# The first transfers of a hybrid encoder layer: gain vector first in ScalarE's queue, first weights behind x's first half in SyncE's, rounded by VectorE

## The chip, the cores and the metric

The kernel runs on one core of a Trainium2 chip. The metric is the device time of one execution in microseconds (us); before the change it is 661.3 us, the median of three runs (661.18 to 662.85).

## The reference

One layer of a hybrid encoder, on 512 tokens of width 2048, in float32:

```python
h = rms_norm(x, norm_w)
proj = jnp.einsum('bsd,de->bse', h, w_in)
q, k, v, g_attn, xr, g_lru = jnp.split(proj, SPLITS, axis=-1)
attn_out = attention_group(q, k, v, q_norm_w, k_norm_w)
lru_out = lru_group(xr, conv_w, conv_b, ...)
mixed = concatenate([rms_norm(attn_out, attn_norm_w) * silu(g_attn),
                     rms_norm(lru_out, lru_norm_w) * silu(g_lru)], axis=-1)
return x + jnp.einsum('bse,ed->bsd', mixed, w_out)
```

Only the beginning matters here: the input x, multiplied column by column by the gain `norm_w`, times a first block of 512 columns of `w_in` (those of `xr`). The factor of the norm that belongs to each token is applied later, to the product.

## The kernel before, in words

Every float32 product is made of three matmuls in a rounded format. A matrix is split into a rounded part (`wh` of the weights, `xh` of x) and a rest (`wl`, `xl`), and the products high times high, high times low and low times high are added up in PSUM. `wsplit` makes the two parts of a weight tile of 128 x 512: ScalarE rounds (`nc.scalar.copy`, L204), VectorE subtracts (L205). `xturn` (L226 to L235) transposes 128 columns of x on TensorE, four 128 x 128 pieces (L230), and from PSUM ScalarE makes `xh` (L232), scaled by the gain column `nw`, and VectorE makes `xl` (L233).

TensorE's order is written out by hand over the whole program. SyncE's is so over the first projection, and those of ScalarE and VectorE over its start. Transfers are issued from the queues of SyncE (SP) and ScalarE (ACT) at the start; `b` is the tile of a chunk of x (256 columns of all 512 tokens, 512 KB), `wr` the tile of raw weights (256 rows of `w_in` by 512 columns, 512 KB). Both firsts are loaded in two halves of 256 KB: SP issues the two halves of x's first chunk, ACT the first weight half, then `norm_w` (8 KB, into `nw_st`), then the second weight half. SP goes on with x's second chunk, the second weights and so on (L223, L193).

`nw_st` holds the gain as 16 rows; `columns` (L176 to L182) turns it with one small transpose on TensorE (L179) and copies the result to `nw` on VectorE (L181).

While the first data are on their way TensorE multiplies ones by ones: `busy(n)` issues n matmuls of 128 x 256 in bfloat16 (L924), whose result nobody reads. These are the fillers. Thirteen (`WARM`) stand ahead of the turn of the gain, six (`WARM2`) between the first transposes of x and the first real matmul. The first weights are consumed by a form of `proj_feat` of its own (L287): four matmuls of `xh` with `wh`, then x's second four transposes, then four with `wl`, four with `xl`, and the same for the second weight half. From the second chunk on the matmuls are those of `mm3` (L145 to L147). L891 and L706 belong to the output projection at the end.

The start is these lines:

```python
busy(WARM)
...
    xs, ws = xload(0, 2), wraw(w_in, 0, C_XR, 2, nc.scalar)
    xc, raw = next(xs), next(ws)
    nc.scalar.dma_start(nw_st, norm_w.rearrange("(k p) -> k p", p=P))
    next(xs), next(ws)
    ...
    columns(nw, nw_st)
    first = [wsplit(raw, 0)]
    xturn(xc, 0)
    busy(WARM2)
```

Of the kernel before, what the change touches and what calls it, by code (L numbers as in the profile page):

```python
# [16 lines left out]
P = 128  # L17
# [19 lines left out]
AHEAD = 600  # L37


WARM, WARM2 = 13, 6  # L40


STEPS = 2
# [5 lines left out]
C_Q, C_K, C_GA, C_XR, C_GL = 0, 1024, 1536, 2560, 3584  # L49
# [6 lines left out]
def hybrid_kernel(  # L56
# [20 lines left out]
    nc = tc.nc  # L77
    xf = x.rearrange("b s d -> (b s) d")
# [29 lines left out]
    def nm(s):  # L108
        cnt[0] += 1
        return f"{s}_{cnt[0]}"  # L110
# [11 lines left out]
    def b4(dt=F32, shape=(P, 2, SEQ)):  # L122
        pool, _, n = work()
        return pools[pool].tile(list(shape), dt, tag="b4", bufs=n, name=nm("b4"))
# [13 lines left out]
    def const(shape, name, dt=F32):  # L138
        return cp.tile(list(shape), dt, tag=name, name=name)

    def f(ap):
        return ap.bitcast(F32)
# [14 lines left out]
    nw_st = const([KT, P], "nw_st")  # L157
# [17 lines left out]
    def columns(dst, src):  # L175

        n = src.shape[0]
        pt = mm()
        nc.tensor.transpose(pt[:, :n], src, ident[:n, :n])  # L179
        with tc.high_priority():  # L180
            nc.vector.tensor_copy(dst, pt[:, :n])  # L181
# [2 lines left out]
        return vec[:, r : r + 1]  # L184


    def wraw(w, r0, c0, nk=1, queue=nc.sync):

        raw = pools["wr"].tile([P, 2, SEQ], F32, tag="wr", bufs=3, name=nm("wr"))
        src = w[r0 : r0 + 2 * P, c0 : c0 + SEQ].rearrange("(k p) e -> p k e", p=P)  # L190
        for k in range(nk):
            ks = slice(k * 2 // nk, (k + 1) * 2 // nk)
            queue.dma_start(raw[:, ks, :], src[:, ks, :])  # L193
            yield raw

    turn_of = [0]

    def wsplit(raw, k):

        turn_of[0] += k  # L200
        pool = pools["wx" if "wx" in pools and turn_of[0] % 2 else "xw"]
        hi = pool.tile([P, SEQ], F32R, tag="wh", bufs=4, name=nm("wh"))
        lo = pool.tile([P, SEQ], F32R, tag="wl", bufs=4, name=nm("wl"))
        nc.scalar.copy(hi, raw[:, k, :])  # L204
        nc.vector.tensor_sub(lo, raw[:, k, :], f(hi))  # L205
        return hi, lo

    def wload(w, r0, c0):
        with tc.high_priority(AHEAD):
            (raw,) = wraw(w, r0, c0)  # L210
            return [wsplit(raw, k) for k in range(2)]
# [2 lines left out]
    xh, xl = [None] * KT, [None] * KT  # L214
    ssq = const([P, NT, KT // 2], "ssq")

    def xload(c, nk=1):

        xc = b4(shape=(P, NT, 2 * P))
        for k in range(nk):  # L220
            ks = slice(k * 2 * P // nk, (k + 1) * 2 * P // nk)
            cs = slice(c * 2 * P + ks.start, c * 2 * P + ks.stop)
            nc.sync.dma_start(xc[:, :, ks], xf[:, cs].rearrange("(t p) d -> p t d", p=P))  # L223
            yield xc

    def xturn(xc, kk):  # L226
        pt = mm()
        for t in range(NT):
            ks = slice(kk % 2 * P, (kk % 2 + 1) * P)
            nc.tensor.transpose(pt[:, t * P : (t + 1) * P], xc[:, t, ks], ident)  # L230
        xh[kk], xl[kk] = x2(), x2()
        nc.scalar.activation(xh[kk], pt, AF.Identity, scale=nw[:, kk : kk + 1])  # L232
        nc.vector.scalar_tensor_tensor(  # L233
            xl[kk], pt, nw[:, kk : kk + 1], f(xh[kk]), op0=ALU.mult, op1=ALU.subtract
        )  # L235
# [8 lines left out]
    def xchunk(c):  # L244
        with tc.high_priority(AHEAD):
            (xc,) = xload(c)
        yield
        with tc.high_priority(AHEAD):
            for k in range(2):
                xturn(xc, 2 * c + k)  # L250
        xsquare(xc, c)
        yield
# [669 lines left out]
    def busy(n):  # L922
        for _ in range(n):
            nc.tensor.matmul(warm[:, : 2 * P], wv[:, :P], wv, start=True, stop=True)  # L924
# [8 lines left out]
    )  # L933
    given = {}
    with tc.high_priority():
        xs, ws = xload(0, 2), wraw(w_in, 0, C_XR, 2, nc.scalar)
        xc, raw = next(xs), next(ws)
        nc.scalar.dma_start(nw_st, norm_w.rearrange("(k p) -> k p", p=P))
        next(xs), next(ws)
        table = const([P, 1], "table")  # L940
        nc.scalar.activation(table, ones[:, :1], AF.Exp)
        columns(nw, nw_st)
        first = [wsplit(raw, 0)]
        xturn(xc, 0)
        busy(WARM2)
    chunks = [xchunk(c) for c in range(1, KT // 2)]
    loads, turns = iter(chunks), iter(chunks)
    for step in proj_feat(C_XR, a1, first, given):
        if step is None:
            with tc.high_priority():  # L950
                first.append(wsplit(raw, 1))
                xturn(xc, 1)
            xsquare(xc, 0)
            next(next(loads), None)
            given[1] = wload(w_in, 2 * P, C_XR)
            continue
        c, e = step
        if (e == 0 or e == 2) and c:
            next(next(loads, iter(())), None)
        if (e, c) == (2, 0) or (e == 1 and c) or (e, c) in ((3, 1), (3, 2)):  # L960
            next(next(turns, iter(())), None)
        if (c, e) == (1, 2):
            given[2] = wload(w_in, 4 * P, C_XR)
            s2.close()
        if (c, e) == (2, 3):
            vec_load()
        if (c, e) == (5, 3):
            columns(vec, vec_st)
        if (c, e) == (KT // 2 - 1, 0):
            with tc.high_priority():  # L970
                xstats()
# [171 lines left out]
```

## Time and profile before

| what | value |
|---|---|
| median of three runs | 661.3 us |
| the profiled execution's own time | 660.07 us |
| its span, first to last instruction | 658.3 us |
| TensorE (PE) busy in the span | 651.0 us |
| VectorE (DVE) busy | 488.2 us |
| ScalarE (ACT) busy | 345.6 us |
| GpSimd (POOL) busy | 92.1 us |
| bytes moved by the DMA engines | 96.17 MB |

PE is TensorE's matmuls and PEld its weight loads, which run beside them. "ACTq" and "SPq" in a row are transfers that the queue of that engine issues. In the rows on DMA, q1 is the queue that SP issues on and q10 that of ACT; both run on the same 16 DMA engines. The 1.77 us between the span and the execution's own time lie outside of what the profile shows.

### The profile page before, as it was taken

What the parts mean: (1) busy time and instruction counts of PE and PEld (TensorE: products, weight loads), DVE (VectorE), ACT (ScalarE), POOL (GpSimd) and SP (SyncE); (2) the same over time, 40 slices, a digit from 0 to 9 for tenths busy, and PEclk for the clock granted to TensorE, in tenths of its full rate; (3) what the DMA queues carried; (4) which work ended last, traced back from release to release, by engine and by line L of the source; (5) the groups of instructions that cost most, each with busy time, mean ns of one, the idle gap of its engine ahead of it and who ended that gap; (6) DMA issues with size and microseconds to landing.
All of it is one profiled execution on the core that took longest, in us unless ns stands there. A gap on an engine that the chain in (4) does not pass through costs nothing.

```text
span 658.3 us, 8625 instructions
## 1 busy us (share of the span) xinstructions
PE 651.0 (99%) x2971; PEld 534.1 (81%) x2971; DVE 488.2 (74%) x843; ACT 345.6 (53%) x639; POOL 92.1 (14%) x121
## 2 busy tenths in 40 slices
PE   8999999999999999999999999999999999999997
PEld 6888888888888888888888888888888888888875
DVE  5879688977687952855955568439958998698994
ACT  3533898489856515453744446435444564334441
POOL 0000000000022301233443335410000000000000
PEclk9999999999999999999999999999999999999999
DMA  8843252322334321346875768663355766585322
GB/s 291 288 131 93 65 167 65 97 64 67 93 121 135 92 69 32 102 143 154 179 186 138 192 141 199 158 140 95 96 177 199 259 210 237 189 293 181 132 77 96
DMA packets 52731, 96.17 MB, mean 146 GB/s; under 512 B 4184, under 2 KB 14544, under 8 KB 52560
## 3 DMA queue, kind: packets, MB, share of 16 engines
q1 hardware_dynamic: 45648, 75.17, 36.1%
q0 software_dynamic: 6720, 19.93, 13.1%
q10 hardware_dynamic: 320, 0.53, 0.3%
q8 instruction: 23, 0.38, 0.2%
q14 instruction: 20, 0.16, 0.1%
HBM read 91.42 MB, written 20.97 MB: 171 GB/s over the span
## 4 chain that ended last, share of the span: by engine, by line
PE 96%; DVE 1%; DMA 1%; issue 1%; ACT 0%; ACTq 0%; DVEq 0%
PE pj L145 20%; PE pj L147 20%; PE pj L146 20%; PE mm L891 12%; PE pj L891 9%; PE mm L145 3%; PE mm L147 3%; PE mm L146 3%; PE mm L575 2%; PE mm L230 1%; PE pj L287 1%; PE mm L523 1%; DMA nw_st<-in_norm_w_dram 1%; DVE ol L706 0%; DMA rw<-in_w_out_dram 0%
## 5 line engine op out<-in xcount | busy, mean ns | idle before, releaser
L145 PE MATMUL pj<-x,wh 128*128 128x512 f32 x376 | 151.2, 402 | 0.0
L147 PE MATMUL pj<-x,wl 128*128 128x512 f32 x376 | 146.9, 391 | 0.0
L146 PE MATMUL pj<-x,wh 128*128 128x512 f32 x376 | 146.6, 390 | 0.0
L204 ACT CAST wh<-wr 128x512 fp32r<-128x512 f32 x144 | 86.5, 617 | 77.1 <-PE pj L147 28.8
L205 DVE TENSOR_TENSOR wl<-wr,wh 128x512 fp32r<-128x512 f32 x144 | 98.0, 701 | 30.3 <-ACT wh L204 30.3
L147 PEld LDWEIGHTS pj<-x,wl 128*128 128x128 f32 x376 | 70.6, 188 | 15.3
L146 PEld LDWEIGHTS pj<-x,wh 128*128 128x128 f32 x376 | 70.8, 188 | 13.9 <-issue 0.5
L145 PEld LDWEIGHTS pj<-x,wh 128*128 128x128 f32 x376 | 70.7, 188 | 13.8 <-issue 0.5
L145 PE MATMUL pj<-wh,x 128*128 128x512 f32 x192 | 75.6, 394 | 0.0
L147 PE MATMUL pj<-wh,x 128*128 128x512 f32 x192 | 75.2, 392 | 0.0
L146 PE MATMUL pj<-wl,x 128*128 128x512 f32 x192 | 75.1, 391 | 0.0
L705 ACT CAST oh<-rw 128x512 fp32r<-128x512 f32 x94 | 54.8, 618 | 31.6 <-PE mm L891 16.5
L706 DVE TENSOR_TENSOR ol<-rw,oh 128x512 fp32r<-128x512 f32 x94 | 60.5, 685 | 9.7 <-ACT oh L705 8.8
L891 PE MATMUL mm<-ol,mh 128*128 128x512 f32 x128 | 50.3, 393 | 0.5 <-DVE ol L706 0.5
L891 PE MATMUL mm<-oh,mh 128*128 128x512 f32 x128 | 50.2, 392 | 0.0
L891 PE MATMUL mm<-oh,ml 128*128 128x512 f32 x128 | 50.2, 392 | 0.0
L577 ACT CAST pt<-mm 128x512 fp32r<-128x512 f32 x32 | 18.8, 586 | 53.1 <-PE mm L575 53.1
L145 PEld LDWEIGHTS pj<-wh,x 128*128 128x128 f32 x192 | 36.1, 188 | 8.1 <-issue 0.2
L146 PEld LDWEIGHTS pj<-wl,x 128*128 128x128 f32 x192 | 36.1, 188 | 8.0 <-issue 0.2
L147 PEld LDWEIGHTS pj<-wh,x 128*128 128x128 f32 x192 | 36.0, 188 | 7.9
L563 DVE TENSOR_REDUCE mx<-mm 128x1 f32<-128x512 f32 x32 | 22.1, 689 | 24.5 <-PE mm L147 24.0
L891 PE MATMUL pj<-ol,mh 128*128 128x512 f32 x96 | 37.9, 394 | 0.0
(207 smaller groups left out, 1112.0 us busy)
## 6 DMA issues: line engine op xcount, KB each, us to landing
wr<-in_w_in_dram SPq DMA_DIRECT2D x71, 512.0 KB, 3.7
rw<-in_w_out_dram SPq DMA_DIRECT2D x63, 256.0 KB, 3.7
ts<-in_w_out_dram POOLq DMA_DIRECT2D x24, 512.0 KB, 6.7
rw<-ts SPq DMA_DIRECT2D x31, 256.0 KB, 4.6
ts<-ts POOLq DMA_DIRECT2D x8, 512.0 KB, 5.3
xt<-in_x_dram SPq DMA_DIRECT2D x8, 512.0 KB, 8.7
b<-in_x_dram SPq DMA_DIRECT2D x7, 512.0 KB, 7.6
out_dram<-xt POOLq DMA_DIRECT2D x12, 256.0 KB, 3.0
```

The lines of the kernel that those rows point to most:

```text
L145: nc.tensor.matmul(acc, lh, rh, start=start, stop=False)
L146: nc.tensor.matmul(acc, lh, rl, start=False, stop=False)
L147: nc.tensor.matmul(acc, ll, rh, start=False, stop=stop)
L204: nc.scalar.copy(hi, raw[:, k, :])
L205: nc.vector.tensor_sub(lo, raw[:, k, :], f(hi))
L230: nc.tensor.transpose(pt[:, t * P : (t + 1) * P], xc[:, t, ks], ident)
L563: nc.vector.tensor_reduce(mx, sc, axis=AX.X, op=ALU.max, negate=True)
L575: nc.tensor.transpose(pt[:, s * P : (s + 1) * P], p[:, s * P : (s + 1) * P], ident)
L577: nc.scalar.copy(pth[:, :, tt], p3)
L705: nc.scalar.copy(hi, src)
L706: nc.vector.tensor_sub(lo, src, f(hi))
L891: nc.tensor.matmul(bank[name, s], lh[:, a, ts_], rh, start=i == 0 and j == 0, stop=i == 7 and j == 2,)
```

## The change

`norm_w` becomes the first transfer of ACT's queue. The second half of x's first chunk goes from SP's queue to ACT's, and the first weight half from ACT's to SP's, behind x's first half; the second weight half stays in ACT's. The first weight half is rounded by VectorE instead of ScalarE; all other weight tiles are rounded by ScalarE as before. The fillers become nine ahead of the turn of the gain, three behind it and four behind x's first transposes, 16 in all and not 19.

```diff
-WARM, WARM2 = 13, 6
+WARM, WARM1, WARM2 = 9, 3, 4
...
-    def wraw(w, r0, c0, nk=1, queue=nc.sync):
+    def wraw(w, r0, c0, queues=(nc.sync,)):
...
-        for k in range(nk):
+        nk = len(queues)
+        for k, queue in enumerate(queues):
...
-    def wsplit(raw, k):
+    def wsplit(raw, k, rounded=nc.scalar.copy):
...
-        nc.scalar.copy(hi, raw[:, k, :])
+        rounded(hi, raw[:, k, :])
...
-    def xload(c, nk=1):
+    def xload(c, queues=(nc.sync,)):
...
-            nc.sync.dma_start(xc[:, :, ks], xf[:, cs].rearrange("(t p) d -> p t d", p=P))
+            queue.dma_start(xc[:, :, ks], xf[:, cs].rearrange("(t p) d -> p t d", p=P))
...
-        xs, ws = xload(0, 2), wraw(w_in, 0, C_XR, 2, nc.scalar)
+        queues = nc.sync, nc.scalar
+        xs, ws = xload(0, queues), wraw(w_in, 0, C_XR, queues)
+        nc.scalar.dma_start(nw_st, norm_w.rearrange("(k p) -> k p", p=P))
         xc, raw = next(xs), next(ws)
-        nc.scalar.dma_start(nw_st, norm_w.rearrange("(k p) -> k p", p=P))
         next(xs), next(ws)
...
-        first = [wsplit(raw, 0)]
+        busy(WARM1)
+        first = [wsplit(raw, 0, nc.vector.tensor_copy)]
         xturn(xc, 0)
         busy(WARM2)
```

ScalarE's instructions at the start of the program before, in order (`wr_141` is the first weight tile, `mm_155` the PSUM tile of x's first transposes):

```order
L193 DMA wr_141<-in_w_in_dram 128x512
L938 DMA nw_st<-in_norm_w_dram 16x128
L193 DMA wr_141<-in_w_in_dram 128x512
L941 ACT_TABLE_LOAD
L941 ACTIVATE table<-ones 128x1
L204 CAST wh_151<-wr_141 128x512
L232 ACTIVATE x_24_160<-mm_155,nw 128x512
```

And in the changed program (`wr_138` is the same weight tile, `b_18_136` x's first chunk, `mm_154` the transposes):

```order
L940 DMA nw_st<-in_norm_w_dram 16x128
L225 DMA b_18_136<-in_x_dram 128x4x128
L194 DMA wr_138<-in_w_in_dram 128x512
L944 ACT_TABLE_LOAD
L944 ACTIVATE table<-ones 128x1
L234 ACTIVATE x_24_159<-mm_154,nw 128x512
L205 CAST wh_175<-wr_138 128x512
```

The gain moved from the second place to the first, half of x stands where the gain stood, and the rounding of the first weight half is gone from ahead of `xh`; what is left is the rounding of the second half.

SyncE's first transfers before (`b_35_195` and `b_47_255` are x's second and third chunk, `wr_197` the second weights):

```order
L223 DMA b_18_139<-in_x_dram 128x4x128 x2
L223 DMA b_35_195<-in_x_dram 128x4x256
L193 DMA wr_197<-in_w_in_dram 128x2x512
L223 DMA b_47_255<-in_x_dram 128x4x256
L223 DMA b_54_291<-in_x_dram 128x4x256
```

And in the changed program:

```order
L225 DMA b_18_136<-in_x_dram 128x4x128
L194 DMA wr_138<-in_w_in_dram 128x512
L225 DMA b_35_192<-in_x_dram 128x4x256
L194 DMA wr_194<-in_w_in_dram 128x2x512
L225 DMA b_47_252<-in_x_dram 128x4x256
```

The second place is now the first weight half, and not x's second half; everything behind it keeps its place.

VectorE's first instructions before:

```order
L181 COPY nw<-mm_148 128x16
L205 TENSOR_TENSOR wl_152<-wr_141,wh_151 128x512
L233 SCALAR_TENSOR_TENSOR x_25_161<-mm_155,nw,x_24_160 128x512
L205 TENSOR_TENSOR wl_179<-wr_141,wh_178 128x512
L233 SCALAR_TENSOR_TENSOR x_34_188<-mm_182,nw,x_33_187 128x512
```

And in the changed program:

```order
L181 COPY nw<-mm_144 128x16
L205 CAST wh_150<-wr_138 128x512
L206 TENSOR_TENSOR wl_151<-wr_138,wh_150 128x512
L235 SCALAR_TENSOR_TENSOR x_25_160<-mm_154,nw,x_24_159 128x512
L206 TENSOR_TENSOR wl_176<-wr_138,wh_175 128x512
```

The cast stands between the gain's copy and the first subtraction. Behind these rows the order of all engines is as it was, apart from the number and the places of the fillers on TensorE.

More of the change, by code (lines that the diff above doesn't have):

```diff
@@ L215, in hybrid_kernel @@
     ssq = const([P, NT, KT // 2], "ssq")
-    def xload(c, nk=1):
+    def xload(c, queues=(nc.sync,)):
         xc = b4(shape=(P, NT, 2 * P))
-        for k in range(nk):
+        nk = len(queues)
+        for k, queue in enumerate(queues):
             ks = slice(k * 2 * P // nk, (k + 1) * 2 * P // nk)
             cs = slice(c * 2 * P + ks.start, c * 2 * P + ks.stop)
-            nc.sync.dma_start(xc[:, :, ks], xf[:, cs].rearrange("(t p) d -> p t d", p=P))
+            queue.dma_start(xc[:, :, ks], xf[:, cs].rearrange("(t p) d -> p t d", p=P))
             yield xc
```

## The prediction

> **What bounds the kernel now.** I read the page first, for who is busy.
>
> ```profile
> span 658.3 us, 8625 instructions
> ...
> PE 651.0 (99%) x2971; PEld 534.1 (81%) x2971; DVE 488.2 (74%) x843; ACT 345.6 (53%) x639; POOL 92.1 (14%) x121
> ```
>
> TensorE is idle for 658.3 - 651.0 = 7.3 us in all. The waits of TensorE between 7 and 640 us, in total, times, and the longest, are one row:
>
> ```profile
> PE mm L891 <- DVE ol L706: 0.5, 1, 0.5
> ```
>
> So from the first real matmul to nearly the end TensorE runs without a gap, and what can be won without less work lies ahead of 7 us or in the tail. The change works ahead of 7 us. There the chain that ended last reads (start, us, what):
>
> ```profile
> 0.72 0.45 ACTq L193
> ...
> 1.20 4.10 DMA nw_st<-in_norm_w_dram
> 5.30 0.14 issue
> 5.43 0.20 PE mm L179
> 5.63 0.60 PE mm L230 x4
> 6.26 0.70 ACT x L232
> ...
> 7.00 1.20 PE pj L287 x4
> ```
>
> The 8 KB of the gain are issued at 1.20, behind the first weight half, land at 5.30, and only then come the turn of the gain, x's transposes, `xh` and at 7.00 the first real matmul. The timeline shows what lies beside and behind this chain (start, us, engine, line, operation):
>
> ```profile
> 0.72 0.45 ACTq L193 DMA_DIRECT2D wr<-in_w_in_dram  x1
> ...
> 1.12 2.96 PE L924 MATMUL mm<-ones 128*128 128x256 bf16 x13 [1.12 <-POOL ones L153]
> ...
> 1.76 0.51 ACTq L193 DMA_DIRECT2D wr<-in_w_in_dram  x1
> ...
> 4.53 0.62 ACT L204 CAST wh<-wr 128x512 fp32r<-128x512 f32 x1 [0.73 <-DMA wr<-in_w_in_dram]
> ...
> 5.76 0.69 DVE L205 TENSOR_TENSOR wl<-wr,wh 128x512 fp32r<-128x512 f32 x1
> ...
> 6.06 0.82 PE L924 MATMUL mm<-ones 128*128 128x256 bf16 x6
> ...
> 7.35 0.62 ACT L204 CAST wh<-wr 128x512 fp32r<-128x512 f32 x1 [0.41 <-DMA wr<-in_w_in_dram]
> ...
> 8.39 1.17 PE L287 MATMUL pj<-x,wl 128*128 128x512 f32 x4
> ...
> 9.26 1.13 ACT L204 CAST wh<-wr 128x512 fp32r<-128x512 f32 x2
> 9.40 1.99 PE L287 MATMUL pj<-x,wh 128*128 128x512 f32 x8
> ...
> 11.68 1.03 PE L230 MATMUL mm<-ident,b 128*128 128x128 f32 x8
> ...
> 13.93 0.39 PE L145 MATMUL pj<-x,wh 128*128 128x512 f32 x1
> ```
>
> The first weight half has landed at about 4.5, the second at 7.35: both casts waited for just that. The weights are early now, and the gain is late.
>
> **The gain first.** What a transfer costs with nothing ahead of it is shown by no row at the start; the nearest are the gain's own 4.10 us with 256 KB ahead of it, and the quick stores of the page, issued on the same kind of queue (KB each, median us to landing):
>
> ```profile
> out_dram<-xt SPq DMA_DIRECT2D x3, 256.0 KB, 2.5
> ```
>
> Issued at 0.72, the gain lands between 0.72 + 2.5 = 3.2 and 0.72 + 4.1 = 4.8. I take 3.2: nothing stands ahead of it, and the row of 2.5 is nearest to that. Nine fillers take until 1.12 + 9 x 0.21 = 3.0 (the spacing of the thirteen: 2.96 less one of 0.42, over 12, is 0.21), so the turn starts at 3.2 at once, and three more fillers end at about 4.0. At the upper end, 4.8, the turn, three fillers and the transposes follow at 5.3 to 5.6, and little of the time won is left: that end stays in the range.
>
> **x's first half** is then what the transposes wait for. Its own landing is not shown, that of the second half is (first and last start; us to landing, of the second alone):
>
> ```profile
> L223 SPq DMA_DIRECT2D b<-in_x_dram x2: 429/463/497, 0.7 to 1.2; - x2
> ...
> DMA to landing us min/median/max: 4.5/4.5/4.5
> ```
>
> The bytes of the two queues from the start to 2.8 us, to 3.6, to 4.0, to 5.0 and, both together, to 5.6 (packets, MB, share of 16 engines):
>
> ```profile
> q10 hardware_dynamic: 17, 0.03, 14.6%
> q1 hardware_dynamic: 179, 0.09, 11.3%
> ```
>
> ```profile
> q10 hardware_dynamic: 114, 0.23, 28.1%
> q1 hardware_dynamic: 282, 0.14, 13.6%
> ```
>
> ```profile
> q10 hardware_dynamic: 141, 0.26, 27.7%
> q1 hardware_dynamic: 474, 0.24, 20.1%
> ```
>
> ```profile
> q1 hardware_dynamic: 1099, 0.58, 38.2%
> ```
>
> ```profile
> DMA packets 1470, 1.07 MB, mean 191 GB/s; under 512 B 64, under 2 KB 1314, under 8 KB 1470
> ```
>
> Both halves of x are 0.524 MB, which q1 had moved at about 4.83; the second landed at 1.2 + 4.5 = 5.7, so 0.87 us pass from last byte to landing. The first half, 0.262 MB, was moved at 4.06 and landed at about 4.9. It was slow because weights competed: from 2.8 to 3.6 q10 moved 0.20 MB and q1 0.05, four to one (2 KB a packet against 512 B, from packets and bytes). Now x's two halves compete with each other, packet for packet alike. With an even half of the 0.50 MB moved by 4.0 the first half is done where it was, and lands at 4.9; with the lead of 0.06 MB that q1 had at 2.8, and half of 0.33 MB/us from there, it is done at 2.8 + 0.17/0.165 = 3.85, and lands at 4.5 to 4.7. Then 0.60 of transposes, 0.70 of `xh` and some 0.1 of issue: `xh` is ready at 5.9 to 6.35, 6.2 in the middle.
>
> **The first weights behind it.** This is the price of the change: they landed at 4.5 and now stand second in q1. Under even sharing both weight halves are done when all four pieces are, 1.05 MB, which the row to 5.6 us puts at 5.55; landing 0.5 (the weights' own delay: 0.26 MB at 4.0, landed 4.53) to 0.87 later is 6.1 to 6.4. With q1 ahead the weights meet the rest of x's second half and take four parts of five: 0.06 MB of x left at 3.85, 0.9 us during which the weights move 0.24, done at 4.8, landed at 5.3 to 5.7. I take 5.8, inside 5.3 to 6.4.
>
> By the Trainium skill (DMA: Bandwidth & Descriptors, Issuing engines are not separate DMA queues) transfers from several engines interleave on the same 16 DMA engines, and issuing from several saves only the issue time. The rows agree as far as bytes go: the sum of both queues stays near 0.33 MB/us whoever issues. Read strictly it leaves the reordering 0.5 us of issue time; that is a rival below, worked out from the rows.
>
> **VectorE's cast.** No row has this shape. The nearest (count, total us, mean ns):
>
> ```profile
> L205 DVE TENSOR_TENSOR wl<-wr,wh 128x512 fp32r<-128x512 f32 x144 | 98.0, 701 | 30.3 <-ACT wh L204 30.3
> ...
> L265 DVE TENSOR_SCALAR k<-ident,rstd 128x128 f32<-128x128 f32 x4 | 0.9, 280 | 1.2 <-POOL rstd L257 1.2
> ...
> L472 DVE COPY k<-k 128x128 f32<-128x128 f32 x2 | 0.4, 222 | 0.0
> ...
> L354 DVE TENSOR_SCALAR c<-lc 128x16 f32<-128x16 f32 x1 | 0.2, 166 | 0.0
> ```
>
> A copy of 128 columns costs 222 ns, and 16 columns of anything about 166, so 0.5 ns a column and 0.41 us for 512; the upper end is the subtraction's 0.70. The copy is nearest in kind: I take 0.41. The saving against ScalarE's 0.62 is 0.2 (or -0.1). It delays `wl` on the same engine, which is due only with the second group of matmuls, 1.39 us behind the first (8.39 - 7.00), and needs 0.69: covered. On ScalarE the first `xh` no longer stands behind a cast that would now wait for weights until 5.8.
>
> **The sum.** First real matmul: the later of `xh` at 6.2 and `wh` at 5.8 + 0.41 + 0.1 = 6.3, so 6.3 against 7.00: 0.7 won. Ends: 5.9 (1.1 won) and 6.4 + 0.5 = 6.9 (0.1 won), or 7.2 with the dear cast (0.2 lost). The four fillers behind the transposes take 0.44 at the late spacing (0.82 less 0.27, over 5, is 0.11) and hide in `xh`'s 0.70.
>
> Is it kept? x's second half lands with the first or a little behind, due at 6.3 + 1.0. The second weights of ACT's queue land by 6.4, earlier than 7.35, due near 9.6. SP's later transfers keep their places, and q1 and q10 carry as many bytes as before, so x's second chunk and its weights come when they came; the weights' cast ran at 9.26 for a matmul at 13.93, now 13.2, and the chunk's transposes go from 11.68 to 11.0. VectorE and ScalarE there wait for TensorE and move along. The tail follows it too. So the span falls by 0.7 to 657.6 and the profiled execution from 660.07 to 659.4; on the median, which lies 1.2 higher, 661.3 becomes **660.6**, 0.1% less.
>
> **The rivals.** *The array is cold at the first matmul.* The fillers' own rows, the first thirteen and then the six (min, median, max ns):
>
> ```profile
> L924 PE MATMUL mm<-ones x13: 395/421/421, 1.1 to 3.7; 128*128 128x256 bf16 x13
> ```
>
> ```profile
> L924 PE MATMUL mm<-ones x6: 272/272/273, 6.1 to 6.6; 128*128 128x256 bf16 x6
> ```
>
> TensorE runs at half its rate (0.21 a filler) until at least 4.1 and at full rate (0.11) by 6.06: 3.0 to 4.9 us of activity were needed. With three fillers fewer and a pause from 4.0 to 4.7 it may not be warm at 6.3; then the real matmuls run that long at half rate and lose 1.5 to 2.5 us: 661.3 - 0.7 + 1.5 to 2.5 = 662.1 to 663.1, slower. It decides as soon as more than 1.4 us of real matmuls run cold, and 0.3% needs 5.4 us of them. Against it: the idle before was longer, 4.08 to 5.43, and did no harm. I give 0.10. By the Trainium skill (TensorE: Matmul & The Clock Gate, What's actually happening) the clock doubles after a busy window of about 3.4 us whose phase runs free of the kernel; that one window would cost half of it, an estimate of 1.7 us, 662.3. The trace agrees on the halving; the phase no row here shows.
>
> *The weights come last.* If they land like the last piece now, 7.35, the first matmul is at 7.35 + 0.5 = 7.85: 0.85 lost, 662.1. For it: they went from first to second. Against: it needs all 1.05 MB and 0.87 of landing to be exceeded by 0.9. With its milder forms, 661.5 to 662.1: 0.10.
>
> *Only issue time is saved.* If a landing hangs on traffic and not on place, the gain lands 4.10 after 0.72 and everything moves by 1.20 - 0.72 = 0.48, or by nothing where something else is late: 660.8 to 661.3. For it: 8 KB took 4.10 though 0.26 MB of q10 were moved at 4.0. I give 0.15.
>
> **How the numbers follow.** The forecast has 0.65: 660.2 to 661.2 by its own ends. The three runs lie 1.7 apart, so a median of three can be off by some 0.6. The range reaches from 659.5 (best end less scatter) to 662.3 (the slow rivals' near parts); about 1 in 7 lies outside. A measurement of this kernel can tell some 0.3%, 2 us: faster than 659.3 needs the best end and luck, 0.06; slower than 663.3 needs a cold array for long, 0.03; the rest, 0.91, is within.
>
> **What would show it.** Right: the turn of the gain at 3.2, x's transposes at 4.5 to 4.9, VectorE's cast near 0.41 us and starting at 5.3 to 6.1, the first L287 at 6.3 and still no idle TensorE behind it. Wrong: the transposes' start set by the gain again, the cast released by the weights above 6.6, four L287 matmuls in about 2.0 us and not 1.20, or a new wait of TensorE between 7 and 30 us.

## The result and the profile after

The changed kernel takes 659.46 us, the median of six runs (659.37 to 659.61); the kernel before 661.58 us in the same comparison (661.17 to 662.85). The ratio is 0.997, with a 95% interval of 0.9958 to 0.9982: faster by 2.1 us, three times the 0.7 that was forecast, and 0.04 us below the 659.5 at which the stated range begins. The profiled execution took 659.61 us. The page of after begins so:

```profile
span 657.8 us, 8619 instructions
...
PE 651.9 (99%) x2968; PEld 534.4 (81%) x2968; DVE 490.5 (75%) x844; ACT 345.5 (53%) x638; POOL 92.3 (14%) x121
```

The span fell by 0.5 us only, from 658.3 to 657.8, and the two profiled executions differ by 0.46 (660.07 and 659.61). So the profiles show a quarter of what the medians show. That gap is what most of the experiments are about. First what the trace of after shows: the chain that ended last, over the first 14 us.

```profile
1.13 2.10 PE mm L926 x9
...
3.33 0.26 PE mm L179
3.58 0.75 PE mm L926 x3
4.34 0.85 PE mm L232 x4
5.19 0.85 PE mm L926 x4
6.04 1.43 PE pj L289 x4
7.47 0.44 PE mm L232 x4
7.91 3.24 PE pj L289 x14
```

The gain's landing is gone from the chain, which is now TensorE's own work from 1.13 us on. The transposes and the fillers take 0.21 us each; they took 0.11 behind the turn of the gain in the profile of before. The timeline of after has the casts and what TensorE did with them:

```profile
4.95 0.43 DVE L205 CAST wh<-wr 128x512 fp32r<-128x512 f32 x1 [1.16 <-DMA wr<-in_w_in_dram]
...
5.97 1.50 PE L289 MATMUL pj<-x,wh 128*128 128x512 f32 x4
...
8.20 0.62 ACT L205 CAST wh<-wr 128x512 fp32r<-128x512 f32 x1 [2.29 <-DMA wr<-in_w_in_dram]
...
13.51 0.19 PEld L146 LDWEIGHTS pj<-x,wh 128*128 128x128 f32 x1 [0.31 <-DVE x L235]
```

The first weight half landed at 4.95, the first real matmul started at 5.97, 1.03 earlier than before. The first four took 1.50 and not 1.20, so some of them ran at half rate. The second weight half came at 8.20, 0.85 later than before, and 0.31 us of waiting for `xl` show up at 13.5. Of the 1.03 us, 0.7 were left at the first matmul of the second chunk (13.24 against 13.93) and 0.5 at the end. The wait for `xl` is booked on a weight load. The matmuls themselves have one wait on record between 7 us and the end, as before:

```profile
PE mm L893 <- DVE ol L708: 0.5, 1, 0.5
```

### The profile page after: what moved, and what is told of

Its sections match the earlier page's. It is cut to its first block, busy times and chain, and to the rows that moved or that the text cites. A ratio compares the mean times of both kernels' runs of the same rounds, so it can differ in the third digit from the quotient of the medians.

```text
span 657.8 us, 8619 instructions
## 1 busy us (share of the span) xinstructions
PE 651.9 (99%) x2968; PEld 534.4 (81%) x2968; DVE 490.5 (75%) x844; ACT 345.5 (53%) x638; POOL 92.3 (14%) x121
## 4 chain that ended last, share of the span: by engine, by line
PE 97%; DVE 2%; issue 1%; ACT 0%; DVEq 0%; POOL 0%; ACTq 0%; POOLq 0%
PE pj L147 20%; PE pj L145 20%; PE pj L146 20%; PE mm L893 12%; PE pj L893 9%; PE mm L145 3%; PE mm L147 3%; PE mm L146 3%; PE mm L577 2%; PE mm L232 1%; PE pj L289 1%; PE mm L525 1%; PE mm L926 1%; DVE ol L708 0%; PE mm L269 0%
## 5 line engine op out<-in xcount | busy, mean ns | idle before, releaser
L206 DVE TENSOR_TENSOR wl<-wr,wh 128x512 fp32r<-128x512 f32 x144 | 99.5, 713 | 32.1 <-ACT wh L205 31.9
```

## The experiments

Each group of runs shared a chip and its runs of the kernel before.

**The kernel before, profiled once more** (no edit).

> The kernel before, unchanged, profiled once more. Two theories on why the change was worth 2.1 us in the medians though the two profiled spans differ by 0.5 us only (658.3 and 657.8). Cold-array theory: in most executions of the kernel before TensorE is still at half rate at the first real matmul, since it idles from 4.1 to 5.4 us; a profile of such an execution shows the six fillers behind x's transposes 0.21 us apart and not 0.11, the first real matmuls at half rate for 1 to 3 us, and a span near 659.5 to 660. Late-gain theory: in most executions the gain vector lands later than 5.30 us, at 6.5 or later, and the first real matmul starts at 8 us or later, at full rate. Both expect times of 661 to 663 with a spread above 1 us, against 659.4 to 659.6 for the changed kernel.

Measured: 661.75 us (661.08 to 662.17), the profiled execution 662.17 with this span and timeline:

```profile
span 660.4 us, 8625 instructions
```

```profile
5.72 0.26 PE L179 MATMUL mm<-ident,nw_st 16*128 16x16 f32 x1 [1.65 <-DMA nw_st<-in_norm_w_dram]
5.91 1.12 PE L230 MATMUL mm<-ident,b 128*128 128x128 f32 x4
...
6.82 1.49 PE L924 MATMUL mm<-ones 128*128 128x256 bf16 x6
...
7.96 2.06 PE L287 MATMUL pj<-x,wh 128*128 128x512 f32 x4
...
9.81 0.86 PE L230 MATMUL mm<-ident,b 128*128 128x128 f32 x4
10.43 1.17 PE L287 MATMUL pj<-x,wl 128*128 128x512 f32 x4
```

The gain landed at 5.6, 0.3 us later than in the first profile: too little for the late-gain theory, which falls. But x's transposes took 1.12 and not 0.66, the six fillers 1.49 and not 0.82, the first four matmuls 2.06 and not 1.20. TensorE ran at half rate until about 10 us. The fillers, meant to cover a wait, became the last wait themselves: `xh` was ready near 7.8, and they held the first matmul until 7.96. At the first matmul with `wl` (10.43 against 8.39) this execution is 2.0 us behind the first profile, and its span is 2.1 longer.

Over all four groups of runs the kernel before was executed 103 times: 29 times in 659.94 to 660.53 us (median 660.18), 72 times in 661.09 to 662.82 (median 661.67), twice between. The profile that the forecast was built on, 660.07, belongs to the smaller group; the new one belongs to the larger. The 12 executions of this run and the six of the comparison above, none of them among the 103, all lie at 661.08 or more. Why the small group is missing there is open.

**More fillers, nothing else.**

```diff
-WARM, WARM2 = 13, 6
+WARM, WARM2 = 19, 6
```

> The kernel before with 19 fillers ahead of the turn of the gain in place of 13, and nothing else: TensorE is then busy from 1.1 to 5.2 us and hardly idles before the gain lands. Cold-array theory: 1 to 1.7 us faster than before (about 660.0), and the spread between runs shrinks to some 0.3 us. Late-gain theory: unchanged, 661 to 662, same spread.

Measured: 660.46 us (660.11 to 660.75) against 661.45, ratio 0.9985 (0.9977 to 0.9994). The start of its timeline:

```profile
5.40 0.20 PE L179 MATMUL mm<-ident,nw_st 16*128 16x16 f32 x1
...
6.02 0.82 PE L924 MATMUL mm<-ones 128*128 128x256 bf16 x6
...
6.97 1.22 PE L287 MATMUL pj<-x,wh 128*128 128x512 f32 x4
```

The first real matmul is where it was in the first profile of before, all transfers are as they were, and yet 1.0 us is won and the spread falls from 2.7 to 0.6 us. So the pause is shown as the cause of the larger group: six useless matmuls in it, and no execution is above 660.75. The profile is of the fastest execution; why the median stays 0.3 us above the small group (660.18) is open.

**The gain first, nothing else.**

```diff
-        xc, raw = next(xs), next(ws)
         nc.scalar.dma_start(nw_st, norm_w.rearrange("(k p) -> k p", p=P))
+        xc, raw = next(xs), next(ws)
```

> The kernel before with the gain vector as the first transfer of ScalarE's queue, and nothing else. The pause of TensorE goes with it, so both theories expect most of the 2.1 us here: 659.3 to 660.3 and a small spread. If the order of x's second half and the weights, or the cast on VectorE, carried the win, it stays near 661.

Measured: 660.03 us (659.65 to 660.58) against 661.45, ratio 0.9982 (0.9974 to 0.9991): 1.4 of the 2.1 us. Its timeline shows why no more:

```profile
5.68 0.62 ACT L204 CAST wh<-wr 128x512 fp32r<-128x512 f32 x1 [1.87 <-DMA wr<-in_w_in_dram]
6.21 0.68 ACT L232 ACTIVATE x<-mm,nw 128x512 fp32r<-128x512 f32 x1
...
6.94 1.21 PE L287 MATMUL pj<-x,wh 128*128 128x512 f32 x4 [0.85 <-ACT x L232]
```

The first matmul starts no earlier than before, now for another reason: the weights, one place further back, land at 5.68, and ScalarE holds x's scaling behind their cast. This is at full rate, and the median is only 0.15 us below the small group of before (660.18): nearly all of the win is the missing pause.

**The changed kernel with one filler.**

```diff
-WARM, WARM1, WARM2 = 9, 3, 4
+WARM, WARM1, WARM2 = 1, 0, 0
```

> The changed kernel with one filler in place of 16. Cold-array theory: the real matmuls start at 5.2 to 5.9 us but at half rate for 2 to 5 us, so 1 to 2.5 us slower than the changed kernel: 660.5 to 662. Late-gain theory: the fillers did nothing but fill, so 659.0 to 659.5.

Measured: 660.94 us (660.08 to 664.91), against 661.45, ratio 0.9997 (0.9983 to 1.001): no difference from before, and 1.5 us above the changed kernel, as the cold-array theory had it. The profile is of the outlier of 664.91; its first matmuls

```profile
5.61 2.07 PE L289 MATMUL pj<-x,wh 128*128 128x512 f32 x4 [0.78 <-ACT x L234]
```

start 0.36 earlier than in after and run at half rate. Its length has another cause as well, one wait of TensorE for GpSimd late in the program:

```profile
PE mm L577 <- POOL k L570: 3.0, 1, 3.0
```

This wait is in no other profile here, and why it came is open. Behind it TensorE ran at half rate once more: the granted clock was 0.50 from 404.7 to 408.0 us.

**The changed kernel again** (no edit), as the base of the next three.

> The changed kernel, unchanged, on the chip and beside the kernels of this group. Both theories (all of the remaining 0.6 us over the kernel with the gain first is an earlier start of the real matmuls; or it is the fillers' new places) expect 659.3 to 659.6, 2.0 us under the kernel before, and a spread below 0.4 us.

Measured: 659.38 us (659.19 to 660.18) against 661.51, ratio 0.9974 (0.9964 to 0.9983), span 657.6. In this execution the first four matmuls started at 5.86 and took 1.20: full rate came sooner than in the profile of after. Two of its rows, for comparison further down:

```profile
5.86 1.20 PE L289 MATMUL pj<-x,wh 128*128 128x512 f32 x4 [0.34 <-ACT x L234]
...
13.35 0.50 PE L146 MATMUL pj<-x,wh 128*128 128x512 f32 x1
```

**The old numbers of fillers.**

```diff
-WARM, WARM1, WARM2 = 9, 3, 4
+WARM, WARM1, WARM2 = 13, 0, 6
```

> The changed kernel with the old fillers, 13, none and 6. Earlier-start theory: thirteen and six fillers at 0.21 us push the first real matmul from 6.0 to about 6.3 us, so 0.2 to 0.4 us slower than the changed kernel, 659.7. Fillers theory: all of the 0.6 us is lost again, 660.0 or more.

Measured: 659.49 us (659.15 to 660.09): 0.1 slower than the changed kernel, inside both spreads, and neither theory's number. With the gain early, the split of the fillers is worth nothing that can be measured. The profile shows why an earlier start need not help:

```profile
5.66 1.19 PE L289 MATMUL pj<-x,wh 128*128 128x512 f32 x4
...
8.15 0.62 ACT L205 CAST wh<-wr 128x512 fp32r<-128x512 f32 x1 [2.54 <-DMA wr<-in_w_in_dram]
...
9.41 1.20 PE L289 MATMUL pj<-x,wh 128*128 128x512 f32 x4 [0.26 <-ACT x L234]
```

The real matmuls began 0.3 us earlier than in after and then waited: the second `xh` stands on ScalarE behind the cast of the second weights, which landed at 8.15.

**ScalarE rounds the first weights.**

```diff
-        first = [wsplit(raw, 0, nc.vector.tensor_copy)]
+        first = [wsplit(raw, 0)]
```

> The changed kernel with the first weight half rounded by ScalarE again. ScalarE then holds the cast ahead of the scaling of x: weights landed at 4.95, cast until 5.6, the high part of x at 6.3, so the first real matmul at 6.3 us and not 6.0. Earlier-start theory: 0.2 to 0.4 us slower, 659.7. Fillers theory: unchanged, 659.4.

Measured: 659.41 us (659.18 to 660.99): no difference in the median. The profile fell on the execution of 660.99:

```profile
4.88 0.62 ACT L205 CAST wh<-wr 128x512 fp32r<-128x512 f32 x1 [1.07 <-DMA wr<-in_w_in_dram]
...
5.41 0.68 ACT L234 ACTIVATE x<-mm,nw 128x512 fp32r<-128x512 f32 x1
...
6.14 2.07 PE L289 MATMUL pj<-x,wh 128*128 128x512 f32 x4 [0.16 <-ACT x L234]
```

The order on ScalarE is as expected, `xh` only 0.17 later than in after: weights that land at 4.9 hardly get in the way of x's scaling, which could start at 5.2 anyway. But this execution ran at half rate until 9.9 us, though TensorE had no pause above 0.2 us since 1.13. So a cold array can come without the pause too; here it is one execution of 11.

**The old queues of x's second half and the first weights**, the gain still first.

```diff
-        xs, ws = xload(0, queues), wraw(w_in, 0, C_XR, queues)
+        xs, ws = xload(0, (nc.sync,) * 2), wraw(w_in, 0, C_XR, (nc.scalar,) * 2)
```

> The changed kernel with x's second half in SyncE's queue and the first weight half in ScalarE's again, behind the gain. The profile of the kernel before with the gain first shows those weights landing at 5.67 us; with the cast on VectorE the first real matmul is at 6.15. Earlier-start theory: 0.1 to 0.3 us slower than the changed kernel. Fillers theory: unchanged, 659.4.

Measured: 659.71 us (659.23 to 661.25), 0.33 slower than the changed kernel.

```profile
6.16 0.43 DVE L205 CAST wh<-wr 128x512 fp32r<-128x512 f32 x1 [2.38 <-DMA wr<-in_w_in_dram]
...
6.73 1.17 PE L289 MATMUL pj<-x,wh 128*128 128x512 f32 x4 [1.35 <-DVE wh L205]
```

In ScalarE's queue behind the gain the weights land at 6.16, in SyncE's behind x's first half at 4.95. By the medians the exchange of the queues is worth 0.3 us once the gain is first, though the two spreads overlap. The profile is of an execution of 660.27, 0.6 above the median.

**The gain second again**, everything else as changed.

```diff
-        nc.scalar.dma_start(nw_st, norm_w.rearrange("(k p) -> k p", p=P))
         xc, raw = next(xs), next(ws)
-        next(xs), next(ws)
+        next(xs)
+        nc.scalar.dma_start(nw_st, norm_w.rearrange("(k p) -> k p", p=P))
+        next(ws)
```

> The changed kernel with the gain as the second transfer of ScalarE's queue again, behind x's second half; everything else as changed. If the gain's place is the main cause, it lands at 5 us or later, TensorE idles from 3.2 us on after nine fillers, and the cold executions come back: 660.5 to 662 with a spread above 1 us. If weights, cast and fillers carry the win, 659.4 to 659.8.

Measured: 662.26 us (661.32 to 662.65) against 661.48, ratio 1.0013 (1.0004 to 1.0021): all of the win is lost and more.

```profile
5.31 0.25 PE L179 MATMUL mm<-ident,nw_st 16*128 16x16 f32 x1 [2.08 <-DMA nw_st<-in_norm_w_dram]
...
6.96 1.06 PE L926 MATMUL mm<-ones 128*128 128x256 bf16 x4
...
7.95 1.50 PE L289 MATMUL pj<-x,wh 128*128 128x512 f32 x4
```

Nine fillers end at 3.2, TensorE pauses for 2.08, and none of the 12 executions is below 661.3. The spread was forecast above 1 us and is 1.3; it no longer holds a group near 660. That may come from the pause, longer than before, but the 12 executions of the kernel before that were taken with its second profile held none either.

**Both weight halves in SyncE's queue.**

```diff
-        xs, ws = xload(0, queues), wraw(w_in, 0, C_XR, queues)
+        xs, ws = xload(0, queues), wraw(w_in, 0, C_XR, (nc.sync,) * 2)
```

> The changed kernel with the second weight half in SyncE's queue too, behind the first: in the changed kernel it lands at 8.0 to 8.2 us, later than the 7.35 of the kernel before, and the profile shows TensorE slowed by it near 8 to 10 us and near 13.4. If that is a limit: landing near 6, the matmuls from the second chunk on 0.2 to 0.4 us earlier, 659.1. If the slow places have other causes: 659.4.

Measured: 659.00 us (658.79 to 659.61) against 661.48, ratio 0.9969 (0.9958 to 0.998): 0.4 below the changed kernel's 659.38, which ran on another chip beside a before of 661.51; the best of all.

```profile
6.38 0.62 ACT L205 CAST wh<-wr 128x512 fp32r<-128x512 f32 x1 [0.49 <-DMA wr<-in_w_in_dram]
...
8.34 1.99 PE L289 MATMUL pj<-x,wh 128*128 128x512 f32 x8
...
13.10 0.39 PE L146 MATMUL pj<-x,wh 128*128 128x512 f32 x1
```

The second weights land at 6.38 and not 8.2, and the wait at 13.5 is gone. It starts its first real matmul at 5.94, no earlier than after, and at the second chunk (13.10) is 0.25 us ahead of the changed kernel's second profile (13.35) and 0.4 ahead of its first (13.51), in which part of the first matmuls ran at half rate.

**The same with x's transposes earlier.**

```diff
-WARM, WARM1, WARM2 = 9, 3, 4
+WARM, WARM1, WARM2 = 9, 0, 4
```

> The same with no fillers between the turn of the gain and x's transposes (9, none and 4). x's first half lands at 3.67 us, the fillers hold the transposes until 4.1. Earlier-start theory: first real matmul at 5.6 us, another 0.2 us, 658.9. Cold-array theory: where full speed comes at a fixed time, an earlier start at half rate wins half of it or nothing: 659.0 to 659.3, with a few slower executions.

Measured: 659.23 us (658.61 to 660.73). Eight executions lie between 658.61 and 659.54, three between 660.52 and 660.73. In the profiled one, of 658.62,

```profile
5.47 1.21 PE L289 MATMUL pj<-x,wh 128*128 128x512 f32 x4
```

the real matmuls start half a microsecond earlier and at full rate. Three fillers fewer buy the earlier start, and three of eleven executions pay more for it, as a cold array would have it. That is not shown: no profile fell on one of the three.

**Two more fillers behind the transposes.**

```diff
-WARM, WARM1, WARM2 = 9, 0, 4
+WARM, WARM1, WARM2 = 9, 0, 6
```

> Both weight halves in SyncE's queue and fillers 9, none and 6. x's transposes start at 3.6 us as with 9, none and 4, but where the array is still at half rate the six fillers last until about 6.0 us and keep TensorE busy as with 9, 3 and 4; where it is at full rate they take 0.6 us and hide. Cold-array theory: the executions near 660.6 that 9, none and 4 had disappear, median 658.8 to 659.0, between the two. If those executions have another cause: again 3 in 11 near 660.6.

Measured: 659.41 us (658.62 to 659.62) against 661.58. No execution of the eight is near 660.6, as expected, but the median is at least 0.4 worse than the forecast and 0.4 worse than that of the kernel with 9, 3 and 4. In the profile, of 659.50, the first real matmuls ran in part at half rate:

```profile
5.75 1.76 PE L289 MATMUL pj<-x,wh 128*128 128x512 f32 x4
```

With eight executions, and the moment of full rate changing from one to the next, I can't say that one is better than the other.

## Why the prediction was right in part

*The mechanism.* The path was the one that was forecast: the gain leaves the chain, TensorE stays dense behind the first matmul, and the only new wait is the 0.31 us at 13.5. Compared with the small group of before (660.18), to which the profile at full rate belongs, the changed kernel (659.46) wins 0.7 us, which is the sum of the prediction. That the sizes agree so well is partly luck, since two terms were off in opposite directions (below).

*The step that failed* is the last of the sum: "on the median, which lies 1.2 higher, 661.3 becomes 660.6". The 1.2 us were taken for scatter that would stay. They are the price of a cold array, paid, by their times, by 72 of 103 executions of before and by none of the 15 of the changed kernel (659.19 to 660.18): 0.7 from the earlier start and some 1.4 from this make 2.1. That the larger group is cold is shown by one profile, of 662.17, and by the two kernels that take the pause away (19 fillers, the gain first); no other execution of that group was profiled.

*The first rival had its sign reversed.* It gave the cold array to the changed kernel, and "the idle before was longer, 4.08 to 5.43, and did no harm" was said of one execution. In the second profile it did harm, and by the times in most executions. The sign "four L287 matmuls in about 2.0 us and not 1.20" came half true in the changed kernel: 1.50 in its first profile, 1.20 in its second. That three runs had a spread of 1.7 us while the profile lay below all of them was there to be read, and was used only to widen the range.

*The gain's landing*: forecast 3.2, from the quickest stores' 2.5 us; measured in after, us from issue to landing, with the issue at 0.72:

```profile
DMA to landing us min/median/max: 2.5/2.5/2.5
```

*The cast*: forecast 0.41, measured 0.43. *The first weights*: forecast at 5.8, measured 4.95, below the lower end of 5.3; x's first half, forecast at 4.5 to 4.9, had landed by 4.1, and at 3.7 where nothing held the transposes (the kernel with one filler). So even sharing of the two queues was wrong, and the first matmul came at 5.97 where 6.3 was forecast. *The second weights* were wrong in the other direction: "by 6.4, earlier than 7.35"; they landed at 8.20. That mis-sized term cost 0.25 to 0.4 us, as the profiles and medians of the kernel with both weight halves in SyncE's queue show. The two errors nearly cancel in the sum.

*The fillers and the cast on VectorE* were costed at nothing to 0.2 us; the runs show 0.1 and 0.03, neither told from nothing. The other rivals: the weights did not come last, and place, not only issue time, decides when the gain lands (2.5 us against 4.1).

## What to carry to other kernels

Before a sum is made from one profile, its time is to be placed among the runs: if it lies at an edge, the first microseconds of a second profile may look different, and a pause of TensorE ahead of the real work is the first suspect. A small transfer that everything waits for belongs ahead of the big ones, and filler matmuls should leave no pause until TensorE runs at full rate. That made cold starts rare here, not impossible. When halves are dealt out to two queues, look at when each piece lands, the last one too.

## What the runs showed of the hardware

*Full rate came 3.1 to 5.9 us after TensorE began to work without a pause, in one execution 8.8 us, and a pause of 1.35 to 1.65 us before that cost most executions time.* Half rate is read from the spacing of the matmuls, 0.21 us a filler and not 0.11. The traces also record the granted clock; at the start that record begins only when the clock becomes full, where the spacing changes, so the profile's clock row shows no half rate there. In the first profile of before it begins at 4.19 us, just behind the thirteenth filler (4.08), and the pause of 1.35 us that followed did no harm. A pause as long, ahead of the first real matmul with the old queues, did none either: full rate had come at 4.58. In the second profile of before it had not come when the fillers ended; TensorE paused until 5.72 and reached full rate at 10.34, 4.6 us later. With the gain second it paused from 3.2 to 5.3 and reached it at 8.63, 3.3 us later. In after, without a pause, it came at 6.66, 5.5 us from the start; where ScalarE rounds the first weights, without one too, at 9.91, 8.8 us from the start. What sets the moment is open.

The Trainium skill (TensorE: Matmul & The Clock Gate, What's actually happening) puts this down to an activity window of about 3.4 us whose phase is free of the kernel. Halving and the change from execution to execution agree, and so do steps in the clock records: full rate lasts 651.95 us in ten profiles and 648.53 us, 3.41 less, in three. The 8.8 us do not fit: two such windows, 6.8 us by an estimate from the page's figure, should hold one that is busy throughout. The page's rule for kernels (Why this matters for your kernels) is to leave no pauses above some 3 us between bursts of matmuls. The kernel with one filler agrees in mid-kernel: behind its wait of 3.0 us the clock was 0.50 for 3.4 us. Ahead of the first full rate the rule is too wide here: filling a pause of 1.35 to 1.65 us with six fillers won 1.0 us.

*Two queues do not share from the moment of issue.* The bytes of after until 3.6 us (packets, MB, share):

```profile
q1 hardware_dynamic: 592, 0.39, 40.0%
q10 hardware_dynamic: 32, 0.01, 1.7%
```

ScalarE's queue q10 had x's second half issued at 1.21, SyncE's q1 the first weights at 1.22, and q1 moved all of its 0.39 MB before q10 moved more than the gain. The second weights, issued at 1.75, landed 6.4 us later. The Trainium skill (DMA: Bandwidth & Descriptors, Queues, rings and completion order) has each DMA engine take turns between the queues packet by packet; no such turn is seen here before 3.6 us. Why q1 went first is open.
